# Feed-forward and down products of a three-layer model: the address distance between stationary and moving operands, stepped by 16 bytes

## The chip, the cores and the metric

One core of one Trainium2 chip runs the whole kernel in one launch. The metric is the device time of one execution in microseconds. The kernel computes in 32-bit floats on 256 tokens (272 with the meta tokens).

## The reference

The input `x` (256 tokens of 2048 features) goes through three layers. Cut to what matters:

```python
# block 1: 16 meta tokens in front, an SSM mixer and an MLA mixer side by side, then
h = h + y @ w_out
h = h + conv_ffn(rmsnorm(h, ffn_norm), w_up, conv_w, conv_b, w_down)      # 2048 -> 2*5504 -> 2048

def conv_ffn(x, w_up, conv_w, conv_b, w_down):
    gate, val = split(x @ w_up, 2)
    gate = sum(conv_w[k] * shifted(gate, k) for k in range(3)) + conv_b
    return (silu(gate) * val) @ w_down

# block 2: two layers, four attention mixers each, then
for l in range(2):
    x = x + rms_norm(mixed @ w_out[l], norm_mix_post[l])
    u = rms_norm(x, norm_mlp_pre[l]) @ mlp_w_up[l]                          # 2048 -> 2*5632
    gate, up = split(conv(u), 2)
    x = x + rms_norm((gelu(gate) * up) @ mlp_w_down[l], norm_mlp_post[l])   # 5632 -> 2048
```

## The kernel before, in words

**Split products.** Each product of 32-bit floats is done as three matmuls on rounded parts. A weight tile is split into `wh` (its value rounded to the matmul's 32-bit format, written by ACT) and `wl` (the rest, a subtraction on DVE), an activation tile likewise into `xh` and `xl` (in the down products `hhh` and `hhl`). `mm3` (lines 630 to 636) then issues `wh` by `xh`, `wl` by `xh` and `wh` by `xl` into the same accumulator. The weight part is the stationary operand, 128 columns; the activation part is the moving operand, 256 columns, or 258 in half of block 1's up product. Each matmul is two records in the profile, the weight load (PEld) and the matmul itself (PE). While one matmul streams its moving operand, the weights of the next are loaded, so TensorE reads two places of the on-chip memory at once.

**The weight stream.** All weights come from DRAM in one list in the order of use, `self.halves` (lines 411 to 425). An entry has 1024 columns for 128 partitions: its address, its width, whether it is held back, and a place `st`. `load_ahead` issues the DMA five entries ahead. `split` (line 540) takes half an entry (512 columns), and writes `wh` and `wl` into tiles of 576 columns at column `st` and on. Eight such pairs of tiles turn, and seven more (`wx`) where `spare` finds room: in block 1's feed-forward and in layer 0's, but not in layer 1's. One pair of 512 columns feeds 12 matmuls.

**Places.** The pools ahead of the weight tiles, the activation tiles (320 words of 4 bytes) and the weight tiles (576 words) all have sizes that are multiples of 64 words. So counted modulo 64 words (256 bytes) all tiles of a kind begin at the same place, and the distance D between stationary and moving operand is the column where the weights begin less the column where the activations begin. `MV, ST = 8, 24` (line 35) are these columns: D = 24 - 8 = 16 words, 64 bytes. In block 1's up product the tile for the gate begins two columns earlier (column 6, 258 wide), the one for the value at column 8: D = 18 and 16 in turn, six matmuls each. In the down products the activations are `hhh` and `hhl`, tiles of 256 words, made by `hsplit` (line 1253). A pad of 8 words ahead of their pool (`padh1` in block 1, `padh2` in layer 0) puts them at place 8, so D = 16 there as well; in layer 1 there is no pad, they begin at place 0, and D = `st`.

**Layer 1 is different.** For the entries from `u` = 128 on (the up product), and from 304 on (the down product), line 421 steps `st` by 8 words (32 bytes):

```python
if l == 1 and u >= 128:
    st = 8 * ((3 + (u - 128) // 8) % 8 if u < 304 else (2 + (u - 304) // 10) % 8)
```

Eight entries are one group of four output tiles, 192 matmuls, in the up product (22 groups); ten entries are five inner tiles, 240 matmuls, in the down product (8 groups, and a shorter one at the end). So D runs through 16, 24, 32, 40, 48, 56, 0, 8, 16, ... in both.

**Order of the work.** A feed-forward is an up product with the convolution, the activation function and the gating on DVE, ACT and POOL beside it (block 1: 43 pairs of output tiles, lines 1206 to 1221, 96 matmuls each; layers 0 and 1: 22 groups of four, lines 1946 to 1953, through `s4`), and then the down product over 43 or 44 inner tiles (`down`, `down_tail`, lines 1259 to 1292), whose last four inner tiles are done column by column with the evacuation beside them. TensorE runs the matmuls in the order in which the program issues them. Ahead of layer 1's feed-forward, its projections and its output product of the mixers use the same tiles and `MV`, `ST`.

Of the kernel before, what the change touches and what calls it, by code (L numbers as in the profile page):

```python
# [20 lines left out]
F32 = mybir.dt.float32  # L21
F32R = mybir.dt.float32r
# [8 lines left out]
L = 272  # L31
LQ = 258
S = 256
XW = 320
MV, ST = 8, 24
# [253 lines left out]
class _Model:  # L289


    def __init__(self):
        self.wr, self.rd, self.alias = {}, {}, {}
# [97 lines left out]
class Kern:  # L391
# [3 lines left out]
    def __init__(self, ctx, tc, A, out, parts, taps):  # L395
        self.ctx, self.tc, self.nc, self.A, self.out, self.taps = ctx, tc, tc.nc, A, out, taps or {}
        nc = self.nc
        self.t = 0.0
        self.sides = []
        self.model = _Model()  # L400
        self.V = _Engine(self, nc.vector, "V")
        self.G = _Engine(self, nc.gpsimd, "G")
        self.H = _Engine(self, nc.scalar, "H")
        self.dclk = 0.0
        self.free = [4, 5, 6, 7]
        self.order = [2, 3, 0, 1]
        self.lead = self.NQ - 2
        self.cap = self.nfree = self.NQ
        self.used = []
        self.locked = False  # L410
        halves = []
        if "b1" in parts:
            halves += [(A["w1"][u // 2, :, 1024 * (u % 2):1024 * (u % 2) + 1024], 1024, 0, ST) for u in range(2 * A["w1"].shape[0])]
        per = A["w2"].shape[0] // 2
        for l in range(2):
            if "l%d" % l in parts:
                for u in range(2 * per):
                    F = 544 if 16 <= u < 24 else 1024
                    st = ST
                    if l == 1 and u >= 128:  # L420
                        st = 8 * ((3 + (u - 128) // 8) % 8 if u < 304 else (2 + (u - 304) // 10) % 8)
                    halves.append((A["w2"][l * per + u // 2, :, F * (u % 2):F * (u % 2) + F], F, 0, st))
                    if u in CMP_AT:
                        halves.append((A["cmpw"][16 * l + CMP_AT.index(u)], 1024, 1, 0))
        self.halves = halves
        self.held = {n for n, x in enumerate(halves) if x[2]}
        self.cq = deque()
        self.xg = None
        self.share = True
        self.nl = self.hp = self.hj = self.ns = self.np = 0  # L430
        self.extra = []
        self.raws, self.ready = {}, deque()

        self.pool("pad0").tile([128, 32], F32, name="pad0")
        self.xp = self.pool("xp")
        self.xh, self.xl = [None] * 16, [None] * 16
        self.wh = self.pool("wh", self.NQ)
        self.wl = self.pool("wl", self.NQ)
        self.wraw = self.pool("wraw", self.NRAW)
        self.pool("pad1").tile([128, 40], F32, name="pad1")  # L440
        p = self.keep = self.pool("keep")
        self.X = p.tile([128, 16, L], F32, name="X")
        self.g2 = [p.tile([128, 65], F32, name="g2_%d" % l) for l in range(2)]
        self.ident = p.tile([128, 128], F32, name="ident")
        self.ones = p.tile([128, 2], F32, name="ones")
        self.mhalf = p.tile([128, 4], F32, name="mhalf")
        self.work = self.pool("work", 2)  
        self.small = self.pool("small", 4)
        pp = self.pool("ps", 1, space=PSUM)
        one = lambda b: pp.tile([128, 512], F32, name="ps%d" % b)  # L450
        self.B = [one(b) for b in range(4)]
        self.P2 = pp.tile([128, 2, 512], F32, name="ps45")
        self.B += [self.P2[:, 0], self.P2[:, 1], one(6), one(7)]
# [4 lines left out]
    def slot(self, name, c, dt=F32R):  # L458

        pool = self.xp if name[0] == "x" else self.yp  # L460
        return pool.tile([128, XW], dt, name="%s%d" % (name, c))[:, MV:MV + L]

    def newx(self, c, at=MV, n=L):
        self.xh[c], self.xl[c] = [self.xp.tile([128, XW], F32R, name="%s%d" % (x, c))[:, at:at + n] for x in ("xh", "xl")]
        return self.xh[c], self.xl[c]

# [784 lines left out]
        return cv  # L1251

    def hsplit(self, pool, hh, k):
        a = self.hx.tile([128, S], F32R, name="hhh")
        b = self.hx.tile([128, S], F32R, name="hhl")
        self.split_act(a, b, hh[:, k], None)
        return a, b

# [390 lines left out]


    def layer(self, l, upd, wx, last):
        nc, A = self.nc, self.A
        V, G, H = self.V, self.G, self.H
        g = self.g2[l]
        g_mix, g_mixp, g_mlp, g_mlpp, dn = g[:, 0:16], g[:, 16:32], g[:, 32:48], g[:, 48:64], g[:, 64:65]
        st = ExitStack()
# [57 lines left out]
        at = ExitStack()  # L1714
# [193 lines left out]
        if not last:  # L1908
            self.spare(wx, 7)
        ff = ExitStack()  # L1910
        if not last:
            self.pool("padh2", 1, ff).tile([128, MV], F32, name="padh")
        self.hx = self.pool("hx2", 5, ff)
        fp = self.pool("f2", 1, ff)
        fp2 = self.pool("f2b", 2, ff)
# [67 lines left out]
        if last:  # L1983
# [3 lines left out]
            while q[0]:  # L1987
                for w, dma in zip(q, (nc.sync, nc.scalar)):
                    if not w:
                        continue  # L1990
                    eng, a, b = w.popleft()
# [435 lines left out]
```

## Time and profile before

| | us |
|---|---|
| runs: median of 2 | 3564.93 |
| runs: lowest, highest | 3563.69, 3566.18 |
| the profiled execution's own time | 3573.9 |
| its span, first to last instruction | 3572.1 |

The profiled execution is 9 us longer than the median of the runs. Its time outside the span is 1.8 us. Its engines: PE (matmuls) busy for 3446.4 us of the span, PEld (weight loads) 3321.2, DVE 2426.4, ACT 1713.0, POOL 501.0. Matmuls are pipelined: one of 256 columns is recorded with some 280 ns, and the next starts well before it ends.

The stages that the change touches lie in the span as follows: block 1's up product from 421 to 914 us and its down product to 1152; layer 0's up product from 1602 to 2090 and its down product to 2341; layer 1's up product from 2793 to 3301 and its down product to 3552.

### The profile page before, as it was taken

The page shows a single profiled execution, that of the slowest core. Times are in us where ns is not written, and L with a number is a line of the kernel's source. Part 1 is how long each engine was busy: PE and PEld are TensorE (multiplying, and loading weights), DVE is VectorE, ACT ScalarE, POOL GpSimd, SP SyncE. Part 2 cuts the span into 40 slices and gives each one's busy share as a digit, 9 for nine tenths or more (in the row PEclk, how much of TensorE's full clock was granted, in tenths as well). Part 3 has the DMA queues.
Part 4 walks back from the last instruction along what each step waited for, and adds up shares of the span by engine and source line. Part 5 has one row for each costly group of instructions (what it writes and reads, how often), then busy time and mean ns, then how long its engine had stood idle before and what let it go on. Part 6 is the DMA issues. An engine that isn't in the chain of part 4 may idle for free.

```text
span 3572.1 us, 70828 instructions
## 1 busy us (share of the span) xinstructions
PE 3446.4 (96%) x27995; PEld 3321.2 (93%) x27995; DVE 2426.4 (68%) x4592; ACT 1713.0 (48%) x3441; POOL 501.0 (14%) x547
## 2 busy tenths in 40 slices
PE   7879999999999999999999999999999999999997
PEld 6768999999999888899999999988889999999997
DVE  7896766666655756558787875565655777777654
ACT  5445544444555545455444444445445444444544
POOL 5652300000001100022000000030001300000002
PEclk9889999999999999999999999999999999999998
DMA  5323555555655654555665565546446355555653
GB/s 175 109 77 107 166 182 184 182 186 189 196 194 165 209 166 158 159 189 166 203 194 190 189 200 185 188 145 210 154 146 196 125 186 189 189 189 189 189 186 122
DMA packets 175022, 618.55 MB, mean 173 GB/s; under 512 B 20224, under 2 KB 24464, under 8 KB 174432
## 3 DMA queue, kind: packets, MB, share of 16 engines
q1 hardware_dynamic: 173488, 612.55, 52.5%
q8 instruction: 219, 3.59, 0.4%
q0 software_dynamic: 336, 0.77, 0.1%
q14 instruction: 115, 0.94, 0.1%
q10 hardware_dynamic: 864, 0.70, 0.1%
HBM read 610.72 MB, written 2.10 MB: 172 GB/s over the span
## 4 chain that ended last, share of the span: by engine, by line
PE 83%; issue 4%; DVE 3%; POOL 1%; DMA 1%; ACT 1%; ACTq 0%; SPq 0%; POOLq 0%; DVEq 0%
PE ps L634 26%; PE ps L635 26%; PE ps L636 26%; PE ps L515 4%; DVE wl L381 1%; DMA wr<-in_w_dram 1%; POOL acc L381 1%; DVE X L381 1%; PE ps L520 1%; DVE xl L381 0%; ACT wh L381 0%; DVE hb L381 0%; DVE xh L381 0%; POOL X L381 0%; DVE y L381 0%
## 5 line engine op out<-in xcount | busy, mean ns | idle before, releaser
L381 DVE TENSOR_TENSOR wl<-wr,wh 128x512 fp32r<-128x512 f32 (+1 forms) x2000 | 1373.7, 715 | 791.0 <-ACT wh L381 787.8
L381 ACT ACTIVATE wh<-wr 128x512 fp32r<-128x512 f32 (+1 forms) x2014 | 1194.6, 623 | 857.8 <-PE ps L636 601.0
L636 PE MATMUL ps<-xl,wh 128*128 128x256 f32 (+2 forms) x4980 | 1402.8, 282 | 2.1 <-DVE xl L381 2.1
L634 PE MATMUL ps<-xh,wh 128*128 128x256 f32 (+2 forms) x4876 | 1387.4, 285 | 13.7 <-ACT xh L381 8.1
L635 PE MATMUL ps<-xh,wl 128*128 128x256 f32 (+2 forms) x4876 | 1376.9, 282 | 8.7 <-DVE wl L381 8.5
L634 PEld LDWEIGHTS ps<-xh,wh 128*128 128x128 f32 x4876 | 927.4, 190 | 27.5 <-ACT xh L381 8.4
L636 PEld LDWEIGHTS ps<-xl,wh 128*128 128x128 f32 x4980 | 948.8, 191 | 2.9 <-DVE xl L381 2.7
L635 PEld LDWEIGHTS ps<-xh,wl 128*128 128x128 f32 x4876 | 927.4, 190 | 14.2 <-DVE wl L381 12.3
L634 PE MATMUL ps<-hhh,wh 128*128 128x256 f32 x1820 | 508.1, 279 | 2.3 <-ACT y L381 1.5
L636 PE MATMUL ps<-hhl,wh 128*128 128x256 f32 x1820 | 507.4, 279 | 0.2 <-DVE hhl L381 0.2
L635 PE MATMUL ps<-hhh,wl 128*128 128x256 f32 x1820 | 507.2, 279 | 0.0
L634 PEld LDWEIGHTS ps<-hhh,wh 128*128 128x128 f32 x1820 | 344.1, 189 | 2.7 <-ACT y L381 1.7
L636 PEld LDWEIGHTS ps<-hhl,wh 128*128 128x128 f32 x1820 | 342.5, 188 | 0.4 <-DVE hhl L381 0.4
L635 PEld LDWEIGHTS ps<-hhh,wl 128*128 128x128 f32 x1820 | 342.7, 188 | 0.0
L381 POOL TENSOR_TENSOR acc<-acc,sq 128x256 f32<-128x256 f32 (+1 forms) x137 | 119.0, 869 | 1152.2 <-ACT sq L381 1147.1
L634 PE MATMUL ps<-yh,wh 128*128 128x258 f32 (+2 forms) x696 | 202.7, 291 | 13.0 <-DVE xl L381 8.7
L381 POOL TENSOR_TENSOR hh<-cv,cv 128x256 f32<-128x256 f32 x88 | 84.5, 961 | 872.3 <-DVE cv L381 840.5
L636 PE MATMUL ps<-yl,wh 128*128 128x258 f32 (+2 forms) x696 | 199.0, 286 | 2.0 <-DVE yl L381 2.0
L635 PE MATMUL ps<-yh,wl 128*128 128x258 f32 (+2 forms) x696 | 198.4, 285 | 0.0
L381 DVE SCALAR_TENSOR_TENSOR cv<-pad,cw,cv 128x256 f32<-128x256 f32 x352 | 180.7, 513 | 13.1
L636 PE MATMUL ps<-xl,wxh 128*128 128x256 f32 x588 | 164.9, 280 | 1.4 <-DVE xl L381 1.4
L381 DVE TENSOR_TENSOR wxl<-wr,wxh 128x512 fp32r<-128x512 f32 x230 | 162.4, 709 | 1.9 <-ACT wxh L381 1.9
(444 smaller groups left out, 4381.8 us busy)
## 6 DMA issues: line engine op xcount, KB each, us to landing
wr<-in_w_dram SPq DMA_DIRECT2D x1105, 512.0 KB, 4.6
wr<-in_cmpw_dram SPq DMA_DIRECT2D x32, 512.0 KB, 5.3
wr<-in_w_dram SPq DMA_DIRECT2D x16, 272.0 KB, 4.8
c2t<-in_c_dram SPq DMA_DIRECT2D x2, 1472.0 KB, 9.7
bc<-in_bc_dram SPq DMA_DIRECT2D x8, 256.0 KB, 3.6
X<-in_hT_dram SPq DMA_DIRECT2D x3, 544.0 KB, 9.7
out_dram<-X SPq DMA_DIRECT2D x5, 256.0 KB, 2.2
s5e<-yh SPq DMA_DIRECT2D x64, 17.0 KB, 2.1
```

Source lines behind the costliest of these rows:

```text
L381: return f(out, *a, **kw)
L515: self.nc.tensor.matmul(out, lhsT, rhs, start=start, stop=stop, skip_group_check=True, **kw)
L520: self.nc.tensor.transpose(out, in_, self.ident[:k, :k])
L634: nc.tensor.matmul(acc, wh, xh, start=start, stop=False, skip_group_check=True)
L635: nc.tensor.matmul(acc, wl, xh, start=False, stop=False, skip_group_check=True)
L636: nc.tensor.matmul(acc, wh, xl, start=False, stop=stop, skip_group_check=True)
```

## The change

The column `st` at which split weights are placed becomes a function of the entry in more stages and in steps of 4 words (16 bytes); the moving operands of layer 1 begin at column 12 in place of 8; the pad ahead of layer 0's `hhh` tiles goes away, and `hsplit` makes wider tiles in layer 1 so that they can begin at column 4.

```diff
         if "b1" in parts:
-            halves += [(A["w1"][u // 2, :, 1024 * (u % 2):1024 * (u % 2) + 1024], 1024, 0, ST) for u in range(2 * A["w1"].shape[0])]
+            halves += [(A["w1"][u // 2, :, 1024 * (u % 2):1024 * (u % 2) + 1024], 1024, 0, ST if u < 80 or u >= 252 else (u - 80) // 4 * 4 % 64) for u in range(2 * A["w1"].shape[0])]
...
                     F = 544 if 16 <= u < 24 else 1024
-                    st = ST
-                    if l == 1 and u >= 128:
-                        st = 8 * ((3 + (u - 128) // 8) % 8 if u < 304 else (2 + (u - 304) // 10) % 8)
+                    st = ST if l == 0 else 28
+                    if u >= 304:
+                        st = 4 * l + (16, 20, 12, 14, 18, 48, 52, 44, 16)[(u - 304) // 10]
+                    elif u >= 128:
+                        st = (4 * ((u - 128) // 8) + st) % 64
...
+        self.mv = MV
...
     def slot(self, name, c, dt=F32R):
 
         pool = self.xp if name[0] == "x" else self.yp
-        return pool.tile([128, XW], dt, name="%s%d" % (name, c))[:, MV:MV + L]
-
-    def newx(self, c, at=MV, n=L):
+        return pool.tile([128, XW], dt, name="%s%d" % (name, c))[:, self.mv:self.mv + L]
+
+    def newx(self, c, at=None, n=L):
+        at = at or self.mv
...
     def hsplit(self, pool, hh, k):
-        a = self.hx.tile([128, S], F32R, name="hhh")
-        b = self.hx.tile([128, S], F32R, name="hhl")
+        o = self.mv - MV
+        a, b = [self.hx.tile([128, S + 16 * o], F32R, name=n)[:, o:o + S] for n in ("hhh", "hhl")]
...
     def layer(self, l, upd, wx, last):
+        self.mv = MV + 4 * l
...
         ff = ExitStack()
-        if not last:
-            self.pool("padh2", 1, ff).tile([128, MV], F32, name="padh")
         self.hx = self.pool("hx2", 5, ff)
```

In distances D, in words modulo 64:

| stage | before | after |
|---|---|---|
| block 1, up (43 groups g) | 18 and 16 | 4g - 6 and 4g - 8 |
| block 1, down | 16 | 16 |
| layer 0, up (22 groups) | 16 | 16, 20, 24, ... |
| layer 0, down (9 groups) | 16 | 16, 20, 12, 14, 18, 48, 52, 44, 16 |
| layer 1, projections | 16 | 16 |
| layer 1, output product of the mixers | 16 | 20 for twelve of the sixteen input tiles (at a fixed column 8), 16 for four |
| layer 1, up (22 groups) | 16, 24, 32, ... | 16, 20, 24, ... |
| layer 1, down (9 groups) | 16, 24, 32, 40, 48, 56, 0, 8, 16 | 16, 20, 12, 14, 18, 48, 52, 44, 16 |

## Rows read from the trace of the kernel before

**Rows 1.** The page: busy us of an engine, share of the span, instructions.
```profile
PE 3446.4 (96%) x27995; PEld 3321.2 (93%) x27995; DVE 2426.4 (68%) x4592; ACT 1713.0 (48%) x3441; POOL 501.0 (14%) x547
```

**Rows 2.** The page: the chain that ended last, by engine, then by line.
```profile
PE 83%; issue 4%; DVE 3%; POOL 1%; DMA 1%; ACT 1%; ACTq 0%; SPq 0%; POOLq 0%; DVEq 0%
PE ps L634 26%; PE ps L635 26%; PE ps L636 26%; PE ps L515 4%; DVE wl L381 1%; DMA wr<-in_w_dram 1%; POOL acc L381 1%; DVE X L381 1%; PE ps L520 1%; DVE xl L381 0%; ACT wh L381 0%; DVE hb L381 0%; DVE xh L381 0%; POOL X L381 0%; DVE y L381 0%
```

**Rows 3.** Stretches by stage: length, TensorE busy (matmuls), granted clock, DMA share, GB/s.
```profile
440.00:900.00 460.00, 460.00 (x3871) 1.00 0.56 186
930.00:1120.00 190.00, 190.00 (x1679) 1.00 0.60 194
1660.00:2080.00 420.00, 420.00 (x3708) 1.00 0.60 195
2092.00:2101.00 9.00, 9.00 (x82) 1.00 0.30 104
2104.00:2314.00 210.00, 210.00 (x1785) 1.00 0.60 191
2825.00:3299.00 474.00, 474.00 (x4002) 1.00 0.56 188
3302.00:3520.00 218.00, 218.00 (x1845) 1.00 0.60 186
2741.00:2781.00 40.00, 40.00 (x342) 1.00 0.67 216
```

**Rows 4.** Stretches inside groups 4 and 6 to 13 of layer 1's up product.
```profile
2894.00:2914.00 20.00, 20.00 (x179) 1.00 0.55 189
...
2939.00:2959.00 20.00, 20.00 (x169) 1.00 0.53 186
2962.00:2982.00 20.00, 20.00 (x171) 1.00 0.54 187
2984.00:3004.00 20.00, 20.00 (x172) 1.00 0.55 186
3007.00:3027.00 20.00, 20.00 (x173) 1.00 0.55 185
3029.00:3049.00 20.00, 20.00 (x171) 1.00 0.54 186
3052.00:3072.00 20.00, 20.00 (x169) 1.00 0.53 181
3075.00:3095.00 20.00, 20.00 (x172) 1.00 0.54 187
3098.00:3118.00 20.00, 20.00 (x172) 1.00 0.53 183
```

**Rows 5.** Stretches inside the first two groups of layer 1's down product.
```profile
3301.00:3327.00 26.00, 26.00 (x232) 1.00 0.63 197
3329.00:3355.00 26.00, 26.00 (x219) 1.00 0.59 186
```

**Rows 6.** Timeline of TensorE in layer 0's down product: start us, us, instruction.
```profile
2101.39 0.28 PE L635 MATMUL ps<-hhh,wxl 128*128 128x256 f32 x1
2101.51 0.32 PE L636 MATMUL ps<-hhl,wxh 128*128 128x256 f32 x1
2101.67 0.28 PE L634 MATMUL ps<-hhh,wxh 128*128 128x256 f32 x1
2101.78 0.28 PE L635 MATMUL ps<-hhh,wxl 128*128 128x256 f32 x1
```

**Rows 7.** Groups of DVE and ACT in layer 1's up product, 2825 to 3299 us.
```profile
L381 DVE TENSOR_TENSOR wl<-wr,wh 128x512 fp32r<-128x512 f32 x338 | 227.8, 719 | 79.7 <-ACT wh L381 79.5
...
L381 ACT ACTIVATE wh<-wr 128x512 fp32r<-128x512 f32 x337 | 198.5, 625 | 126.1 <-PE ps L636 117.6 <-DMA wr<-in_w_dram 5.6 <-DVE wl L381 2.3
```

## The prediction

> **What bounds the kernel now.** I read the engine shares first: TensorE is busy for 96% of the span and the next engine, DVE, for 68% [rows 1]. The chain of work that ended last says the same: 83% of it is TensorE, nearly all of that in the three matmuls of a split product, lines 634 to 636 [rows 2]. So what matters is how far apart two such matmuls start, their pitch; there are about 19,000 of them in the three feed-forwards. A duration of 276 or 282 ns is no help, since matmuls overlap. I take the pitch from the table of stretches: the length of a stretch by the count in brackets. (A stretch also counts the two or three matmuls that had begun before it; in those of 20 us I take 2 off, in long ones it doesn't matter.)
>
> The stretches of one stage each give [rows 3]: block 1's up product 460 us / 3871 = 118.8 ns; its down product 190 / 1679 = 113.2; layer 0's up 420 / 3708 = 113.3; layer 0's down 9.0 / 80 = 112.5 at first and then 210 / 1785 = 117.6; layer 1's up 474 / 4002 = 118.4; layer 1's down 218 / 1845 = 118.2. The granted clock is 1.00 in all of them, the upper of its two levels (2.4 GHz), so it isn't the clock. The work per matmul is the same in the last five, 256 columns. What differs is the distance D between the addresses of stationary and moving operand, modulo 64 words of 4 bytes: 16 words everywhere up to layer 1, whose up and down products step it by 8 words per group.
>
> Layer 1 is thus a measurement of D. In its up product, group by group [rows 4]: D = 48: 20 us / 177 = 113.0; 0: 20 / 167 = 119.8; 8: 118.3; 16: 117.6; 24: 117.0; 32: 118.3; 40: 119.8; 48: 117.6; 56: 117.6. The next eight groups repeat the last eight values. Its down product starts at D = 16 with 26 / 230 = 113.0 and has 26 / 217 = 119.8 in the next group, at 24 [rows 5]. Two things follow. The pitch changes at the border of a group and comes back with D, so the distance does act. And D = 16 and D = 48 each have two values, 113 and 117.6: the stream falls into one of them and keeps it. Layer 0's down product shows the fall: four starts at 2101.39, 2101.51, 2101.67 and 2101.78 us, of which one comes 160 ns after the last [rows 6]; before it the pitch is 113, and for 200 us after it 117.6, at one and the same D.
>
> By the Trainium skill ("SBUF — State Buffer", section "Who interferes with whom") TensorE's two read ports, one for the moving operand and one for loading weights, are independent, and "PE and ACT never wait on anyone". By that the distance would cost nothing and the change would bring 0. The trace disagrees: the 113.0 and 119.8 ns above are the same instructions on the same clock. That reading is a rival below.
>
> **The change part by part.** All pitches are those of the paragraphs above; no instruction is added or removed, and only addresses move.
>
> (1) Layer 0's up product, D = 16 in all 22 groups before, becomes 16, 20, 24, ... in steps of 4. The trace shows no odd multiple of 4. Bounds are the fastest and the slowest pitch of any D, 113.3 and 119.8. I take the mean of the only stage whose D is stepped, layer 1's up product: 118.4, because half of the new distances are in it and the other half lie between them. The first two groups are ruled by stalls at the start of the stage, so 20 groups x 192 matmuls = 3840, and 3840 x (118.4 - 113.3) = +19.6 us. Bounds 0 and +25.
>
> (2) Layer 1's up product steps by 4 in place of 8, both operands moved by 16 bytes. The same mean: 0. Bounds: all at 113.3 gives -20 us, all at 119.8 +6.
>
> (3) Block 1's up product, D = 18 and 16 for its two column tiles, becomes 4g - 6 and 4g - 8 over 43 groups. It stands at 118.8 with half its matmuls at 258 columns; two columns more at 2.4 GHz are 0.8 ns, so a stepped stage would have 118.4 + 0.4 = 118.8. So 0. Bounds: 113.7 gives -20 us, 120.2 gives +5.
>
> (4) Block 1's down product keeps D = 16, but comes from D = 32 in place of 16. Whether it starts at 113.2 or at 117.6 hangs on how the stream arrives. Layer 1 shows both: from 8 to 16 it stays at 117.6 [rows 4], from 56 to 16 it comes to 113.0 [rows 5]. Bounds 0 and 1900 x 4.4 = +8.4; I take the middle, +4.
>
> (5) Both down products get D = 16, 20, 12, 14, 18, 48, 52, 44, 16 by groups of 240 matmuls. In layer 0 D = 16 before: the nearest row to any of these is 117.6, the longer value at 16 and 48, so 0; bounds 1785 x (113.3 - 117.6) = -7.7 and 1785 x 2.2 = +3.9. In layer 1 the groups averaged 118.2; one at 113.3 and seven at 117.6 average 117.1, so 1845 x -1.1 = -2. Bounds -9 and +3.
>
> (6) In layer 1 the output product of the mixers has twelve of sixteen input tiles at a fixed place, so their D goes from 16 to 20. It stands at 40 / 342 = 117.0 [rows 3]; some 576 matmuls, by the pitches 113.3 and 119.8 bounds of -2.1 and +1.6, taken as 0.
>
> (7) ACT and DVE now write the split weights at places that are multiples of 16 bytes, in two groups of 8, where they were multiples of 32. Per 12 matmuls (1.42 us) they need 625 and 719 ns [rows 7], and over that stage DVE waits 80 us of 474 for ACT. That hides up to some 15% on each write; a slower write shows only at the start of a stage, where TensorE waits for it. Taken as 0, bounds 0 and +3. The padding tile that goes away and the wider tiles in layer 1 cost nothing but space.
>
> Sum: 19.6 + 4 - 2 = +21.6 us. On the profiled execution, 3573.9, that is 3595.5. The median of the runs is 3564.9, 9 us below the profiled execution, so 3586.5: **3587 us**, 0.6% slower. Nothing late takes over: TensorE stays the bound at every step, since a higher pitch gives the others more time.
>
> **The rivals.** *A: the short pitch reaches to neighbouring distances, and the change is faster.* If 113.3 holds within 4 words of 16 and of 48, six of the sixteen residues have it. Layer 0's up product then loses 14 x 192 x 5.1 = 13.7; layer 1's gains six groups net, 5.9; the down products gain 7.7 and 9. Sum -9: 3556 us. For it: 16 and 48 are the only distances that ever have the short pitch, and nothing measured is nearer than 8 words. Against it: at 16 the stream stays at 117.6 in two of three visits in layer 1, and once out of it nothing brings it back but a lucky entry or a stall. It decides at layer 0's second group, D = 20: if that has 113, A holds.
>
> *B: the new distances are the bad ones.* All stepped groups at 119.8 (seen at 0, 24 and 40) and block 1's down product at 117.6: 25 + 6 + 5 + 8.4 + 3.9 + 3 + 1.6 = +53, 3618 us. For it: three of eight distances reach that pitch. Against it: five don't, and the sequence passes over those too.
>
> *C: the distance does nothing.* Layer 1 would then take longer because it has no spare weight buffers while layer 0 has, and the time stays at 3565. Against it: within layer 1 the buffers are the same in every group, and the pitch moves with D. (The rule of the Trainium skill quoted above would come out here as well.)
>
> **How the numbers follow.** The forecast has 0.58, with 3574 to 3600 as its own range: part (4) by 4 either way, and the stepped stages' mean by 1 ns over some 9000 matmuls. A has 0.2, B 0.15, C 0.05, a slower write that shows 0.02. From 3556 to 3606 about 8 in 10 lie inside: half of A and most of B are left out. Faster or slower by over 2% (71 us), about what a measurement of this kernel can tell from no change, is out of reach of every sum here: even all bounds together give -59 and +56. So faster 0.01, within 2% 0.97, slower 0.02.
>
> **What would show it.** In the profile after, layer 0's up product at about 118.4 ns, with the pitch changing every 192 matmuls and equal to that of layer 1's up product at equal D; block 1's up product near 118.8; block 1's down product at one of 113.2 and 117.6 throughout; the first down group at 113, the rest between 113 and 120; DVE and ACT with the same durations within a few ns. I would be wrong if layer 0's up product stays at 113.3 at D = 20, or if a pitch below 113 or above 121 appears at a distance that no group has now.

## The result, and the profile after

| | before | after |
|---|---|---|
| runs: median of 2 | 3564.93 | 3602.45 |
| runs: lowest, highest | 3563.69, 3566.18 | 3601.03, 3603.86 |
| the profiled execution's own time | 3573.9 | 3601.03 |
| its span | 3572.1 | 3599.2 |

The ratio is 1.0105 (95%: 1.0062 to 1.0149), +37.5 us: slower, though by less than 2%. Between the two profiled executions it is +27.1 us. Both figures matter below.

The page after gives the engines as before [rows 1], TensorE with the same 27,995 matmuls and 27 us more:

```profile
PE 3473.2 (96%) x27995; PEld 3347.8 (93%) x27995; DVE 2427.1 (67%) x4592; ACT 1714.6 (48%) x3441; POOL 501.4 (14%) x547
```

The stretches by stage of the kernel after, in the order of [rows 3] (length, TensorE busy and matmuls, granted clock, DMA share, GB/s):

```profile
440.00:900.00 460.00, 460.00 (x3868) 1.00 0.56 185
930.00:1120.00 190.00, 190.00 (x1615) 1.00 0.57 187
1660.00:2110.00 450.00, 450.00 (x3806) 1.00 0.59 188
2140.00:2345.00 205.00, 205.00 (x1744) 1.00 0.59 191
2855.00:3328.00 473.00, 473.00 (x4010) 1.00 0.56 188
3331.00:3548.00 217.00, 217.00 (x1851) 1.00 0.59 188
2760.00:2810.00 50.00, 50.00 (x430) 1.00 0.66 210
```

Length by count again: block 1's up 118.9 ns (before 118.8), its down 117.6 (113.2), layer 0's up 118.2 (113.3), its down 117.5 (117.6), layer 1's up 118.0 (118.4), its down 117.2 (118.2), its output product 116.3 (117.0). The clock is 1.00 as before. Two stages moved, and both left 113. In microseconds, from the start of a stage's first split matmul to the start of its last, the same matmuls in both traces:

| stage (matmuls) | before | after | difference |
|---|---|---|---|
| block 1 up (4128) | 493.2 | 493.7 | +0.5 |
| block 1 down (2064) | 237.5 | 245.7 | +8.2 |
| layer 0 up (4224) | 490.5 | 512.0 | +21.5 |
| layer 0 down (2112) | 250.6 | 250.3 | -0.3 |
| layer 1 up (4224) | 510.3 | 510.0 | -0.3 |
| layer 1 down (2112) | 251.1 | 249.6 | -1.5 |

The sum is +28.2, of +27.1 in the span. (The expectations below count the waits beside a stage too: a layer's up product is some 6 us longer there, layer 0's down product some 9.) To find the same in one group, stretches inside layer 0's up product after, at D = 36, 16 and 20:

```profile
1739.00:1759.00 20.00, 20.00 (x172) 1.00 0.58 182
...
1988.00:2008.00 20.00, 20.00 (x179) 1.00 0.56 181
2010.00:2030.00 20.00, 20.00 (x171) 1.00 0.59 190
```

and inside layer 1's, at the same three distances:

```profile
2947.00:2967.00 20.00, 20.00 (x179) 1.00 0.57 191
...
3196.00:3216.00 20.00, 20.00 (x179) 1.00 0.56 182
3219.00:3239.00 20.00, 20.00 (x171) 1.00 0.56 193
```

With 2 taken off each count: 117.6, 113.0, 118.3 ns in layer 0, and 113.0, 113.0, 118.3 in layer 1. (One matmul more or less in such a count is 0.7 ns.) D = 20 is at 118.3 in both, between 113.0 at 16 and, by the starts of the matmuls in the next group, 117 at 24. And D = 36 differs: 117.6 in layer 0, 113.0 in layer 1, at equal distance. Layer 1's operands both lie 4 words further on; the sixth run below takes that up.

The groups of DVE and ACT in layer 1's up product, against [rows 7]:

```profile
L381 DVE TENSOR_TENSOR wl<-wr,wh 128x512 fp32r<-128x512 f32 x339 | 228.1, 718 | 80.5 <-ACT wh L381 80.0
...
L381 ACT ACTIVATE wh<-wr 128x512 fp32r<-128x512 f32 x339 | 199.4, 625 | 124.1 <-PE ps L640 108.9 <-DMA wr<-in_w_dram 7.8 <-DVE wl L381 6.7
```

718 and 625 ns, as 719 and 625 before: the finer places cost the writers nothing.

### The profile page after: what moved, and what is told of

It reads as the page before. It is cut to its first block, busy times and chain, and to the rows that moved or that the text cites. A ratio compares the mean times of both kernels' runs of the same rounds, so it can differ in the third digit from the quotient of the medians.

```text
span 3599.2 us, 70828 instructions
## 1 busy us (share of the span) xinstructions
PE 3473.2 (96%) x27995; PEld 3347.8 (93%) x27995; DVE 2427.1 (67%) x4592; ACT 1714.6 (48%) x3441; POOL 501.4 (14%) x547
## 4 chain that ended last, share of the span: by engine, by line
PE 84%; issue 4%; DVE 3%; POOL 1%; ACT 1%; DMA 0%; SPq 0%; POOLq 0%; ACTq 0%; DVEq 0%
PE ps L638 27%; PE ps L639 26%; PE ps L640 26%; PE ps L519 4%; DVE wl L381 1%; POOL acc L381 1%; DVE X L381 1%; PE ps L524 1%; DVE xl L381 0%; DMA wr<-in_cmpw_dram 0%; DVE hb L381 0%; DVE xh L381 0%; ACT wh L381 0%; POOL X L381 0%; DMA wr<-in_w_dram 0%
## 5 line engine op out<-in xcount | busy, mean ns | idle before, releaser
L638 PE MATMUL ps<-hhh,wh 128*128 128x256 f32 x1820 | 510.3, 280 | 2.3 <-ACT y L381 1.5
## 6 DMA issues: line engine op xcount, KB each, us to landing
wr<-in_w_dram SPq DMA_DIRECT2D x1105, 512.0 KB, 4.6
wr<-in_cmpw_dram SPq DMA_DIRECT2D x32, 512.0 KB, 5.0
```

The source lines that it names most:

```text
L638: nc.tensor.matmul(acc, wh, xh, start=start, stop=False, skip_group_check=True)
```

## The experiments

All times are medians of runs on one chip, beside runs of the kernel before on the same chip; its medians there are 3567.8 us (25 runs, for the first four experiments), 3574.5 (13, for the fifth to seventh), 3573.3 (21, for the eighth and ninth), and 3570.0 and 3566.0 (11 each, for the tenth and eleventh).

**1. Layer 0's up product back to one distance.** The kernel after, with

```diff
-                    elif u >= 128:
+                    elif u >= 128 and l == 1:
```

> The changed kernel with layer 0's up product put back to one distance, D = 16. Theory T (the pitch is set by the distance, with two pitches at 16): that stage goes back from 518 to about 497 us, some -21 us, with 113.3 ns in its groups; block 1 and layer 1 keep the changed kernel's pitches; layer 0's down product may start differently, by up to 8 us either way. Time about 3581 us. Rival C (the distance does nothing, something else in the changed kernel costs the time): the stage stays at 518 us and the time at 3602.

Measured 3577.8 us (10 runs), 1.0021 (1.0002 to 1.0039). Its stretches in block 1's down product and layer 0's up product:

```profile
930.00:1120.00 190.00, 190.00 (x1615) 1.00 0.54 187
1660.00:2095.00 435.00, 435.00 (x3841) 1.00 0.59 198
```

Layer 0's up product is back at 113.3 ns and at 492.1 us, 19.9 less than after; block 1's down product stays at 117.6. So the stepping of this one stage is over half of the loss.

**2. Block 1's up product back to its two distances.** The kernel after, with

```diff
-... ST if u < 80 or u >= 252 else (u - 80) // 4 * 4 % 64) for u in range(2 * A["w1"].shape[0])]
+... ST) for u in range(2 * A["w1"].shape[0])]
```

> The changed kernel with block 1's up product put back to D = 18 and 16. Theory T with a memory of the way in: the up product itself hardly moves (494 to 493 us), but its down product, whose own distance was never changed, goes from 117.8 back to 113.3 ns, -8 us; time about 3594. Rival C: nothing moves, 3602. Rival (the down product's 8 us are chance from run to run, not the way in): 117.8 stays or comes at random.

Measured 3590.1 us (10 runs), 1.0058 (1.0041 to 1.0076). Its stretches in block 1's down product and layer 0's up product:

```profile
930.00:1120.00 190.00, 190.00 (x1679) 1.00 0.57 195
1660.00:2095.00 435.00, 435.00 (x3680) 1.00 0.56 186
```

Block 1's down product is at 113.2 again (237.3 us, 8.4 less than after), though the edit doesn't touch it: its own D is 16 in both kernels. What differs is the distance from which the stream comes. A stage at D = 16 takes one of the two pitches by what came ahead of it, and here keeps it.

**3. One distance everywhere.** The kernel before, without layer 1's steps, and with block 1's two distances moved to 50 and 48:

```diff
-... 1024, 0, ST) for u in range(2 * A["w1"].shape[0])]
+... 1024, 0, ST if u < 80 or u >= 252 else 56) for u in range(2 * A["w1"].shape[0])]
...
-                    if l == 1 and u >= 128:
-                        st = 8 * ((3 + (u - 128) // 8) % 8 if u < 304 else (2 + (u - 304) // 10) % 8)
...
-        if not last:
+        if True:
             self.pool("padh2", 1, ff).tile([128, MV], F32, name="padh")
```

> The kernel before with layer 1 no longer stepped (D = 16 in its up and down products, with the pad of 8 words ahead of its hhh tiles as in layer 0), and block 1's up product held at D = 50 and 48 in place of 18 and 16. Theory T: layer 1's up product has one pitch in all its groups, 113.3 (-20 us) or 117.8 (-2 us), and its down product one of the same two (-9 or 0); block 1's up product about 116.7 ns in place of 118.9, -9 us, as the changed kernel had in its two groups at this distance. Time between 3525 and 3560. Rival C (layer 1 takes longer because it has no spare weight buffers): layer 1's up product stays at 118.4 and the time within 10 us of 3565.

Measured 3537.2 us (4 runs), 0.9905 (0.9869 to 0.9940). Its stretches in block 1's up product, layer 0's up product, and layer 1's up and down products:

```profile
440.00:900.00 460.00, 460.00 (x3881) 1.00 0.56 186
1630.00:2080.00 450.00, 448.95 (x3949) 1.00 0.58 197
...
2830.00:3270.00 440.00, 440.00 (x3884) 1.00 0.57 194
3285.00:3495.00 210.00, 210.00 (x1856) 1.00 0.61 197
```

Layer 1's products run at 113.3 and 113.1 ns from end to end, in 490.5 and 241.6 us against 510.3 and 251.1: all of layer 1's longer time came from its steps. Block 1's half of the edit missed: 118.5 ns, 492.0 us, 1.1 less than before. Block 1's pitch is thus not that of D = 48 as another stage had it.

In this profile a stall in layer 0's down product is left. In the timeline two starts are 147 ns apart (unrounded; some 113 is the rule up to there):

```profile
2101.50 1.05 POOL L381 TENSOR_TENSOR hh<-cv,cv 128x256 f32<-128x256 f32 x1 [3.31 <-ACT wxh L381]
2101.87 0.96 DVE L381 TENSOR_TENSOR hhl<-hh,hhh 128x256 fp32r<-128x256 f32 x1
...
2102.97 0.31 PE L634 MATMUL ps<-hhl,wxh 128*128 128x256 f32 x1
2103.11 0.28 PE L632 MATMUL ps<-hhh,wxh 128*128 128x256 f32 x1
```

The subtraction for `hhl` lies beside a POOL product and takes 0.96 us; TensorE waits for it, and the rest of the stage runs at 117.6. It is the stall of [rows 6], at the same matmul.

**4. Other constant distances.** The kernel before, with D = 0 in layer 0's up product and 48 in its down product and in both of layer 1's (`hhh` begins at column 0 there, so 48 is its D):

```diff
-                    if l == 1 and u >= 128:
-                        st = 8 * ((3 + (u - 128) // 8) % 8 if u < 304 else (2 + (u - 304) // 10) % 8)
+                    if u >= 128:
+                        st = (8, 56)[l] if u < 304 else (56, 48)[l]
```

> The kernel before with each stage held at another single distance: layer 0's up product at D = 0, its down product at 48, layer 1's up and down products at 48. Theory T: layer 0's up product at 120.0 ns in every group, +26 us; layer 0's down product and layer 1's two products each at one of 113.3 and 117.8, so -8 to 0, -20 to -2 and -9 to -1. Time between 3555 and 3590, with the first term to be read in the profile. Rival C: layer 0's up product stays at 113.3 and layer 1's at 118.4.

Measured 3590.1 us (10 runs), 1.0057 (1.0034 to 1.0081). Its stretches in these four stages:

```profile
1650.00:2110.00 460.00, 460.00 (x3835) 1.00 0.55 185
2125.00:2340.00 215.00, 215.00 (x1827) 1.00 0.56 189
2860.00:3320.00 460.00, 460.00 (x3908) 1.00 0.55 188
3330.00:3540.00 210.00, 210.00 (x1855) 1.00 0.58 196
```

D = 0 gives 119.9 ns through a whole stage (517.4 us, 27 more than before), with nothing stepped. D = 48 gives 117.7 in two stages and 113.2 in the third. So it is the distance that acts, not the stepping; and 48, like 16, has two values.

**5. The stall removed.** The third kernel, with the first three `hsplit` issued one group earlier and handed to `down`:

```diff
+            if t == NP2 - 2:
+                dq = deque(self.hsplit(fp2, hh, i) for i in range(3))
...
-        self.down(fp2, hh, NP2, tg[0])
+        self.down(fp2, hh, NP2, tg[0], dq)
```

> As e3, and in layers 0 and 1 the first three pairs of hhh and hhl are made ahead of the last group of the up product, as block 1 does, so that no matmul of the down product waits for one. No distance changes against e3. Theory M (the pitch at 16 is kept until something disturbs the stream; in layer 0's down product the disturbance is the one wait of some 47 ns for hhl at its third inner tile): that stage has no wait there, stays at 113.3 ns, and is some 8 us shorter than e3's, 260 to 252; time about 3529. Rival (117.8 in that stage comes from the place of its tiles, behind the spare weight buffers that layer 1 doesn't have): the wait goes and 117.8 stays, time 3537.

Measured 3538.7 us (10 runs), 0.9931 (0.9897 to 0.9965). The stretches in layer 0's up and down products:

```profile
1630.00:2080.00 450.00, 450.00 (x3961) 1.00 0.60 197
2090.00:2300.00 210.00, 210.00 (x1855) 1.00 0.59 194
```

In the profiled execution the down product keeps 113.2 ns and takes 241.9 us against 251.2 in the third run's profile, as a stall's removal should give. But the median didn't move against the third kernel, since the runs fall into clusters: six at 3530 to 3539, three at 3564 to 3570, one at 3586. About 28 us lie between the first two. That is 4.4 ns for the 4224 + 2112 matmuls of layer 0's feed-forward, so I took it that the up product too is sometimes entered at 117.7; the eighth run shows it.

**6. The same distances at other places.** The kernel after, with layer 1's operands both moved back by 4 words, so that in the up and down products D is as after and the places are those of layer 0. (The edit also takes layer 1's output product ahead of them from D = 20 back to 16.)

```diff
-                    st = ST if l == 0 else 28
+                    st = ST
...
-                        st = 4 * l + (16, 20, 12, 14, 18, 48, 52, 44, 16)[(u - 304) // 10]
+                        st = (16, 20, 12, 14, 18, 48, 52, 44, 16)[(u - 304) // 10]
...
-        self.mv = MV + 4 * l
```

> The changed kernel with both operands of layer 1 moved back by 16 bytes: the same distances in its up and down products as the changed kernel has, at other places. In the changed kernel D = 24 and 36 gave 117.3 and 118.3 ns in layer 0, 116.7 and 113.6 in layer 1. Theory P (the place counts beside the distance): layer 1's up product now repeats layer 0's pitches group by group, 117.3 at 24 and 118.3 at 36. Theory M (distance and the way in alone): it keeps 116.7 and 113.6. Time between 3595 and 3610 by both.

Measured 3602.0 us (one run). Stretches at D = 36 and 20 in layer 0, and at 36 and 20 in layer 1:

```profile
1733.00:1753.00 20.00, 20.00 (x169) 1.00 0.56 178
...
2005.00:2025.00 20.00, 20.00 (x171) 1.00 0.58 191
2945.00:2965.00 20.00, 20.00 (x169) 1.00 0.54 183
...
3217.00:3237.00 20.00, 20.00 (x171) 1.00 0.56 190
```

The two layers now agree within one matmul in every such stretch, at five distances; D = 36 in layer 1 has gone from 113.0 to 119.8. The 113.0 wasn't chance: runs 1 and 2, whose layer 1 is that of the kernel after, have it again at 36 (20 us / 177), and layer 0 of run 2 has its 117.6 again (20 / 170). So the place of the operands may count beside their distance. It isn't shown, because the way into the stage was moved as well, by the output product. And a pitch isn't fixed by distance and place: layer 0's own group at D = 36 has 172 matmuls in the profile after and 169 here, with nothing of layer 0 edited, and the eighth run has a clearer case.

**7. Short detours.** The third kernel, with one entry (24 matmuls) in eight at another distance in layer 0's up product, two groups for each of ten distances:

```diff
+                    if l == 0 and 144 <= u < 304 and u % 8 == 0:
+                        st = (8 + (24, 56, 0, 8, 32, 40, 48, 20, 12, 36)[(u - 144) // 16]) % 64
```

> As e3, but in layer 0's up product the first 24 matmuls of each group from the third on are at another distance (24, 56, 0, 8, 32, 40, 48, 20, 12, 36, two groups each), the other 168 at 16. Theory M: the 168 have one pitch throughout, 113.3 or 117.8, kept from the way in, and at least some of the ten distances leave 117.8 behind, so the stage is 3 to 15 us longer than e3's 497. Rival (each distance has its pitch and the stream forgets): all 168s have 113.3 as they have in e3, and only the 24s cost, at most 20 x 24 x 6.7 ns = 3 us.

Measured 3536.7 us (one run); the up product takes 496.7 us, 6.2 more than in the third run. Stretches ahead of the first detour, then, in the 168 matmuls at D = 16, behind the first by 24, the first by 0, the second by 8, and the first by 32:

```profile
1637.00:1654.00 17.00, 17.00 (x146) 1.00 0.86 288
1658.00:1675.00 17.00, 17.00 (x153) 1.00 0.56 176
1747.00:1764.00 17.00, 17.00 (x146) 1.00 0.61 191
...
1814.00:1831.00 17.00, 17.00 (x147) 1.00 0.57 188
1836.00:1853.00 17.00, 17.00 (x153) 1.00 0.56 190
```

Less 2, that is 118.1, 112.6, 118.1, 117.2, and 112.6 again. Twenty-four matmuls decide over the 168 behind them, though these are at one and the same D: over whole groups the stream stays at 117.8 behind both detours by 0 and both by 8, and is at 113.3 behind every other. In this execution the detours thus moved the stream between the two values of D = 16, in both directions; runs 9 and 11 show that they don't always.

**8. The early split in the kernel before.** Only the edit of the fifth run, on the kernel before.

> The kernel before, unchanged in its distances, with the first three pairs of hhh and hhl of layers 0 and 1 made ahead of the last group of the up product. Theory M (what the wait of some 150 ns pitch at the third inner tile leaves behind is a matter of chance, 113.3 or 117.8, and that is part of the spread of the runs): no wait there, layer 0's down product at 113.3 in every execution; its profile is 8 to 9 us shorter in that stage than before's (259.7 us), and the median of the runs 3 to 9 us below that of before on the same chip. Rival (chance between runs has other sources): the profile's stage is shorter, the median within 2 us of before's.

Measured 3569.3 us (10 runs), 0.9998 (0.9971 to 1.0026): no change clear of noise, though the medians are 4.0 us apart. Its profiled execution, one of three at 3590 to 3597, has layer 0's up and down products at

```profile
1660.00:2110.00 450.00, 450.00 (x3823) 1.00 0.58 188
2118.00:2325.00 207.00, 207.00 (x1760) 1.00 0.59 187
```

117.7 and 117.6 ns: at D = 16 all through, without a stall, and with both stages at the longer pitch from the second group of the up product on. The down product isn't shorter (251.1 us against 250.6), so the expected gain didn't come. The other seven runs are at 3563 to 3571. The kernel before on that chip has 17 of 21 runs at 3562 to 3580 and four at 3586 to 3597. So it seems that the pitch is settled at the start of the up product in each execution anew, and the early split has no say there.

The same profile has layer 1's up product with addresses and order unedited up to its last group. At D = 16 and 24, where the kernel before has 117.6 and 117.0 ns (2984 and 3007 us in [rows 4]), it shows

```profile
3007.00:3027.00 20.00, 20.00 (x178) 1.00 0.60 204
3029.00:3049.00 20.00, 20.00 (x169) 1.00 0.58 190
```

113.6 and 119.8 ns. So one program's pitch can differ between executions at 24 as well as at 16, at equal distance and place.

**9. One detour as a repair.** The fifth kernel, with one entry at D = 32 in the output product and one in the up product of each layer:

```diff
+                    st = 40 if u in (96, 136) else ST
```

> As e5, with 24 matmuls at D = 32 at the start of the mixers' output product and of the second group of the up product, in both layers; all else stays at 16. e5 has 117.8 in the output product (some 700 matmuls in each layer) and in that second group. Theory M with the way back seen in e7 (24 matmuls at 32 brought the stream from 117.8 to 113.3): the output products go to 113.3 behind the 24, some 3 us in each layer, and the second groups too, 0.8 us in each; the profile some 7 us shorter than e5's in these stretches. Rival (the way back in e7 was the chance of that place): 117.8 stays in the output products, and the time is e5's.

Measured 3545.0 us (10 runs), 0.9914 (0.9878 to 0.9950), in two clusters: five at 3526 to 3533, five at 3557 to 3567. The profiled execution, of the second cluster, has in layer 0's up product, layer 1's output product and layer 1's up product

```profile
1660.00:2105.00 445.00, 445.00 (x3780) 1.00 0.58 187
...
2735.00:2775.00 40.00, 40.00 (x355) 1.00 0.69 219
2860.00:3290.00 430.00, 430.00 (x3797) 1.00 0.58 194
```

117.7, 113.3 (40 us / 353) and 113.2 ns. Layer 0's output product stays long as well (45 us / 382 = 117.8). So the expected way back came in layer 1's output product and not in layer 0's: a single detour by 32 doesn't reliably bring the stream back, although one did so in the seventh run, behind a detour by 8.

**10. Ten different detours.** The fifth kernel, with

```diff
+                    if 136 <= u < 216 and u % 8 == 0:
+                        st = (8 + (24, 56, 32, 40, 20, 36, 12, 24, 56, 32)[(u - 136) // 8]) % 64
```

> As e5, with 24 matmuls at another distance at the start of groups 1 to 10 of the up products of layers 0 and 1: 24, 56, 32, 40, 20, 36, 12, 24, 56, 32; all else at 16. In e5 and e9 the executions fall into two clusters, 3526 to 3539 and 3557 to 3586 us, and a profile of the second has 117.8 in all groups of an up product. Theory B (in e7 the stream left each of these distances at 113.3, and from 117.8 it came back behind 24 and behind 32): whatever the start, the groups behind are at 113.3, the detours cost some 0.15 us each, 3 us in all; the runs are one cluster from 3528 to 3545. Rival (what follows a detour is chance again, or the start decides for the stage): two clusters as before, with runs over 3555 in 3 to 5 of 10, or a profile with 117.8 behind the detours.

Measured 3537.8 us (6 runs, 3535.65 to 3539.03), 0.9904 (0.9882 to 0.9925): one cluster. In the profiled execution both up products are at 113.2 ns behind the detours:

```profile
1860.00:2090.00 230.00, 230.00 (x2032) 1.00 0.59 191
...
3040.00:3270.00 230.00, 230.00 (x2032) 1.00 0.57 192
```

This profile doesn't show a way back, since layer 0's stream has the short pitch already behind the first detour (16 us / 141 = 113.5). That several detours bring it back rests on the six runs.

**11. Five detours by 24.** The fifth kernel, with

```diff
+                    st = 32 if u in (96, 100, 136, 144, 152) else ST
```

> As e5, with 24 matmuls at D = 24 at the start of groups 1, 2 and 3 of the up products of layers 0 and 1, and twice near the start of the mixers' output products of both; all else at 16. Theory B24 (the distance 24 alone brings the stream back): one cluster of runs, 3527 to 3537 us; the output products at 113.3 behind the detours (3 us less in each layer than e5's 117.8), both up products at 113.3 from group 2 on. Rival (which distance brings it back depends on the way in, so three equal detours are not enough): a second cluster over 3555 again, or the output products stay at 117.8.

Measured 3532.8 us (6 runs, 3525.1 to 3536.6), 0.9892 (0.9874 to 0.9909), faster than the kernel before. Stretches in layer 0's output product, behind the first, second and third detour of its up product, over the rest of it, and behind the first and second detour of layer 1's:

```profile
1525.00:1585.00 60.00, 60.00 (x532) 1.00 0.67 212
1640.00:1652.00 12.00, 12.00 (x105) 1.00 0.95 320
1658.00:1676.00 18.00, 18.00 (x156) 1.00 0.55 174
1681.00:1698.00 17.00, 17.00 (x152) 1.00 0.58 193
1702.00:2088.00 386.00, 386.00 (x3409) 1.00 0.59 193
2820.00:2836.00 16.00, 16.00 (x139) 1.00 0.70 218
2841.00:2858.00 17.00, 17.00 (x152) 1.00 0.61 209
```

The output product is at 112.8 ns; in the kernel before and in the runs above layer 0's is at 117 to 118. In its up product, two detours leave the stream at the longer pitch (12 us / 103 = 116.5, 18 / 154 = 116.9), the third brings 113.3 (17 / 150), and it stays (386 / 3409 = 113.2). In layer 1 the first leaves 116.8 (16 / 137), and the second brings 113.3 (17 / 150). The runs with several detours have 12 of 12 executions in the short cluster, the fifth and ninth 11 of 20. That the eleventh beats the tenth, or either of them the constant distances of the third (0.9905) and fifth (0.9931), isn't shown by the times, as the intervals overlap; what differs is the share of executions in the long cluster.

## Why the prediction was right, and where it wasn't

The direction, the place and the wide range held: 3587 with 3556 to 3606 was forecast, 3602.45 measured. The narrower range that the prediction gave its own sum, 3574 to 3600, was passed, and by the median alone rival B (3618) was as near as the forecast. It is the profile that bears the sum out: +28.2 by stages against +21.6, nearly all in the two stages named. By its steps:

- **(1) Layer 0's up product, +19.6:** +21.5 in the profiles, and run 1 takes 19.9 back. The new distances don't lie between their neighbours as I took it: by the starts of the matmuls, in the second pass of layer 0's groups over them, 20 has 118.8 between 113.3 at 16 and 117.3 at 24, and 28 has 120.0 between 117.3 at 24 and 118.6 at 32. The mean of the groups is 118.3, not much from the 118.4 that was taken over from layer 1, and the two groups at the start cost more as well.
- **(2), (3), (5), (6), (7):** 0, 0, 0 and -2, 0, 0 against -0.3, +0.5, -0.3 and -1.5, 0.7 ns on some 576 matmuls, and no longer writes. All hold as sums. In layer 1's down product that is partly luck: seven groups were put at 117.6, and they have 113.4 to 120.0, which comes out alike.
- **(4) Block 1's down product, +4:** +8.2. The step that failed is "I take the middle". The quantity has two values and no middle, and run 2 shows that its way in decides: from 18 and 16 it comes to 113.2, from 34 and 32 to 117.6.
- **The step from the profile to the median** is the larger miss. I took 9 us off the sum because the median of the two runs was 9 us below the profiled execution. After, its runs and its profiled execution agree, and nothing is 9 us lower. The terms give +28.2, and with those 9 us about the +37.5 of the runs. What they were is made likely by the fifth run: layer 0's down product takes 241.9 us at the short pitch and 250.6 in the profiled execution of before, which had the long one, 8.7 apart. Run 8, in which that stall is gone, has no run between 3571 and 3590, where the kernel before on the same chip has 12 of 21. But no execution of before at 3564 was profiled, so this is argued and not shown. If it is so, the kernel before gets the short pitch at D = 16 by chance in part of its executions, and the kernel after has given up that chance.
- **The signs.** The pitches of block 1 and the means of the up products came as listed. One sign didn't: layer 0's groups should equal layer 1's at equal D, and at 36 they have 117.6 and 113.0. So the premise that the distance alone sets a pitch, outside 16 and 48, failed, without moving the sum. And the limit of 121 ns for a new distance was touched: by the starts of the matmuls, three groups of block 1's up product (D = 62 and 60) have 121.4, with half of their matmuls at 258 columns.

Rival A falls on its own test: D = 20 has 118.3 ns in both layers. A neighbour can have the short pitch (36 in layer 1), but not reliably. Rival B falls, as the layers' stepped up products average 118.2 and 118.0 and not 119.8, though its value for block 1's down product was the right one. Rival C falls with run 4: the same matmuls of layer 0's up product, in the same buffers, take 113.3 ns at D = 16 and 119.9 at D = 0. The rule of the Trainium skill quoted in the prediction ("SBUF — State Buffer", section "Who interferes with whom"), by which the change would bring 0, doesn't hold for these matmuls.

Open are what in the on-chip memory makes the pitch, what at the start of an up product decides between the two pitches at D = 16, and why block 1's up product is at 118.5 to 118.9 in every version; its distances were changed twice, and its mean moved by 0.3 ns at most; constant single ones weren't tried. Open too is whether the place of the operands counts beside their distance.

## What to carry to other kernels

Where TensorE is the bound and streams back to back, read its pitch (length by count) stage by stage, before and beside any other figure: here the granted clock was 1.00 in either case and TensorE was busy throughout, and some 28 us lay in 113 against 118 ns. Hold stationary and moving operands at one place that has shown the short pitch, not at a changing one, and look at several executions, since the same program can be at either pitch. When a term of the forecast has two values, name what chooses between them, or carry both; and don't move a sum by the gap between a profiled execution and a median before knowing which stage makes that gap.

## What the runs showed of the hardware that wasn't expected

- The pitch of a 256-column matmul depends on the addresses of its operands to 16 bytes: 113.3 ns at D = 16 and 119.9 at D = 0 over nearly all of an up product (run 3 and run 4), and 113.0 and 118.3 in neighbouring groups at D = 16 and 20 (after), at equal granted clock.
- At one distance it can have either of two values and keep it for thousands of matmuls (3409 in run 11, 3823 in run 8); in run 8 the down product behind is at the same pitch, 117.6. At 24, too, one program had 117.0 in one execution and 119.8 in another (before and run 8).
- One start that comes late, 147 or 160 ns behind the last in place of 113, stood at the change from the short to the long pitch (run 3, before), and 24 matmuls at another distance can change it (run 7). Neither need do so: behind a first detour layer 0's stream stayed at the long pitch in runs 9 and 11, and in the kernel after a start some 190 ns behind the last, in layer 0's down product, left the stream where it was, at 14 us / 124 = 112.9 behind it.
- Absolute places may count as well: D = 36 had 113.0 ns, and 119.8 when both operands were moved by 4 words (run 6). As the distance in the product ahead was changed with them, this isn't shown.
